# Gated attention of a two-layer decoder: scores inside blocks of 32 keys by small matmuls instead of 128-wide ones

## The chip, the cores and the metric

One core of a Trainium2 chip runs the whole forward pass of a two-layer decoder trunk for one sequence of 512 tokens (model width 1024). The metric is the device time of one execution in microseconds (us), given as the median of several runs. The trace that is read below is that of one profiled execution.

The engines are called by the names of the profile: PE is the matmul engine (PEld its loading of the stationary operand), DVE the vector engine, ACT the scalar engine, POOL a further vector engine that is almost unused here, and SP the queue that issues most DMAs. Each engine takes its instructions in order.

## The reference, cut to what matters

Layer 0 mixes tokens by gated linear attention with 4 heads, layer 1 by latent attention; each mixer is followed by a SwiGLU network, and every part is preceded by an RMS norm. What the change touches is the first mixer and the statistics of the norms:

```python
def gla_chunked(q, k, v, log_a):          # q, k, log_a (B,S,H,128), v (B,S,H,256)
    ...
    b = jnp.cumsum(gi, axis=-2)
    ...
    diff = b[:, :, :, None, :] - b[:, :, None, :, :]
    decay = jnp.exp(jnp.where(causal, diff, -jnp.inf))
    attn = jnp.einsum('bhik,bhjk,bhijk->bhij', qi, ki, decay)
    o_intra = jnp.einsum('bhij,bhjv->bhiv', attn, vi)

def rmsnorm(t, g):
    y = tf * lax.rsqrt(jnp.mean(tf * tf, axis=-1, keepdims=True) + EPS)
```

The score of a query i on a key j is a sum over 128 channels of q times k times a product of gates between j and i, one gate for each token and channel.

## The kernel before

All activations are kept transposed: channels on the 128 partitions, 512 tokens along the free dimension. Most matrix products are done in three matmuls on operands split into a high and a low part (`mm3`, L175 to L177), each 128 by 128 by 512. Weights arrive by SP in units of 128x1024 (`raw`), are rounded by ACT to `wh` (L161), and DVE subtracts to get `wl` (L169); three buffers of each rotate. In the first 265 us DVE also makes the modulation vectors of both layers from the weights `adaw` (L132): each is 512 KB, two buffers rotate, and DVE multiplies and sums one in L136 (`junk`).

**Scores of the gated attention.** For each head there is a tile `dg` of 128 keys by 4 times 128 queries: the diagonal blocks of the score matrix. It is filled in levels s = 1, 2, 4, ..., 64 (`LEVELS`). At level s, keys in an even group of s tokens meet queries in the odd group right after it, so that q and k, which `decay` (its two products are L580 and L581) multiplies by the gates of the groups after each level, carry the right product of gates. `head_setup` makes the diagonal itself: four matmuls of 128 keys by 128 queries, of which a product with the identity leaves the diagonal (L530). `level` (L548) does levels 1 to 16 with four matmuls a head, each of 128 keys by the 64 odd queries of a tile of 128 tokens (L556), and DVE copies the wanted entries through a mask `lm` (`copy_predicated`, L570). Levels 32 and 64 are done by `blocks` (L537): matmuls of only s keys by s queries (L542), whose output starts at partition b, and whose result DVE copies whole (L545). These operands are full fp32, and the trace has two records ("pieces" below) for each such matmul of the program.

**Order.** PE runs in an order that is written out by hand (`manual_schedule`). After the diagonals of heads 0 to 2 comes one unit of the v product, then the diagonal of head 3, then level 1 for the 4 heads, then a filler of 24 dense matmuls, level 2 for the 4 heads, a filler, and so on (`fill`). The fillers are units of the v product (`v_units`) and tiles of the gate (`r_tile`). DVE, ACT and SP are ordered by a scheduler from priorities and its own costs. ACT's order is by hand in the logs of the gates and in the first stretch of the program alone.

**Statistics of a norm.** `rstd_stats` (L216) sums squares over the channels: for each 128 tokens a matmul whose stationary operand is the tile `acc` of squares (128 tokens wide) and whose moving operand is one column of ones (L225); DVE then works out the inverse root on 128x4 numbers (L228, L203 to L212), and `rstd_spread` broadcasts it (L240). There are 15 such matmul groups: seven over all 512 tokens (first norm, four heads, `ckv`, `cq`), six over half the tokens, and two in the last norm over half the tokens with two operands each.

Of the kernel before, what the change touches and what calls it, by code (L numbers as in the profile page):

```python
# [18 lines left out]
P = 128  # L19
# [3 lines left out]
NT = S // P  # L23
# [17 lines left out]
FF_CHUNKS = ((0, 8), (8, 15), (15, 22))  # L41

LEVELS = (1, 2, 4, 8, 16, 32, 64)


C_ADAB = 0
# [10 lines left out]

K_ID = 0
K_CAUS = 128
NK_COL = 256  # L60

MAGIC = 12582912.0
TWO_PI = 6.283185307179586476925286766559
# [17 lines left out]
def trunk(ctx: ExitStack, tc: tile.TileContext, t: dict, out: bass.AP):  # L81
# [12 lines left out]
    def R(name, dt=F32, cols=S):  # L94
        return ring.tile([P, cols], dt, tag="ring", name=name, bufs=NRING)
# [7 lines left out]

    cols = cst.tile([P, NC_COL], F32, name="cols")
    kc = cst.tile([P, NK_COL], F32, name="kc")
    lm = cst.tile([P, 7 * 64], I32, name="lm")
    cact = cst.tile([P, D], F32, name="cact")
    x = [cst.tile([P, S], F32, name=f"x{k}") for k in range(KD)]
    ident = kc[:, K_ID:K_ID + P]
# [376 lines left out]
    def log_gates():  # L486
# [30 lines left out]
        for hd in range(H):  # L517
            et = R("et")
            nc.scalar.activation(out=et[:, :off], in_=tt[hd][:, :off], func=AF.Exp, scale=1.0 / TAU)
            heads[hd] = dict(e1=e1[hd], et=et, offs=offs)  # L520

    def head_setup(hd):
        d = heads[hd]
        qs, kr = qk[("q", hd)], qk[("k", hd)]
        dg = R("dg")
# [9 lines left out]
        d.update(kr=kr, qf=qf, dg=dg)  # L535

    def blocks(ps, kr, qf, dg, s):  # L537

        lo = range(0, P, 2 * s)
        for i in range(NT):  # L540
            for b in lo:
                nc.tensor.matmul(ps[b:b + s, i * s:(i + 1) * s], lhsT=kr[:, i * P + b:i * P + b + s],  # L542
                                 rhs=qf[:, i * P + b + s:i * P + b + 2 * s], start=i == 0, stop=i == NT - 1)
        for b in lo:
            nc.vector.tensor_copy(out=dg[b:b + s].rearrange("p (t a) -> p t a", t=NT)[:, :, b + s:b + 2 * s],  # L545
                                  in_=ps[b:b + s, :NT * s].rearrange("p (t a) -> p t a", t=NT))

    def level(hd, li, s):  # L548
        d = heads[hd]
        kr, qf, dg = d["kr"], d["qf"], d["dg"]  # L550
# [8 lines left out]
        na = 64 // s  # L559
        o = dg.rearrange("p (t a b s) -> p t a b s", t=NT, b=2, s=s)[:, :, :, 1, :]  # L560
        mk = lm[:, li * 64:(li + 1) * 64]
        dd = ps[:, :256]
        if 1 < s < 64:
            mk = mk.rearrange("p (a s) -> p a s", s=s)[:, None, :, :].to_broadcast([P, NT, na, s])
            dd = dd.rearrange("p (t a s) -> p t a s", t=NT, s=s)
        else:
            o = o.rearrange("p t a s -> p t (a s)")
            mk = mk[:, None, :].to_broadcast([P, NT, 64])
            dd = dd.rearrange("p (t a) -> p t a", t=NT)
        nc.vector.copy_predicated(out=o, mask=mk, data=dd)  # L570

    def decay(hd, s):
# [493 lines left out]
def _pack(inp):  # L1066
# [44 lines left out]
    kcv = np.zeros((P, NK_COL), np.float32)  # L1111
    kcv[:, K_ID:K_ID + P] = np.eye(P, dtype=np.float32)
    kcv[:, K_CAUS:K_CAUS + P] = np.where(np.arange(P)[None, :] > np.arange(P)[:, None], np.float32(-1e30), 0)
    d["kc"] = kcv
    j = np.arange(P)[:, None]
    lms = []
    for s in LEVELS:
        a = np.arange(64)[None, :] // s
        lms.append(((j // (2 * s) == a) & ((j // s) % 2 == 0)).astype(np.int32))
    d["lm"] = np.ascontiguousarray(np.concatenate(lms, axis=1))  # L1120

    gw = f("gla_w_in")[0]
# [62 lines left out]
```

## Time and profile before

| | us |
|---|---|
| median of 3 runs | 1202.94 (1202.93 to 1205.04) |
| the profiled execution, device time | 1200.87 |
| its span in the trace | 1199.1 |
| PE busy | 1168.8 (97% of the span) |
| DVE busy | 733.4 (61%) |
| ACT busy | 414.3 (35%) |
| POOL busy | 15.9 (1%) |

A matmul's end is modelled in the trace, so the pace of PE is read from the start of one row to the start of the next. A row with "x32" merges 32 neighbours of one line, and its length reaches to the modelled end of the last. The text in brackets at a row's end is the idle time of the engine before it and what ended it.

### The profile page before, as it was taken

To read this page: it belongs to the slowest core of one execution; us is meant where nothing else is said; L and a number is where in the kernel's file an instruction comes from. 1 tells how busy PE (TensorE), PEld (TensorE's weight loads), DVE (VectorE), ACT (ScalarE), POOL (GpSimd) and SP (SyncE) were. 2 spreads that over 40 slices of the span, in tenths; PEclk is the share of its full clock that TensorE was granted. 3 is DMA by queue.
4 is the path that set the end of the run, shared out by engine and by line. 5 is a ranking of instruction groups with operands and counts; after the bars stand their busy time and mean duration, and the time that the engine had idled before them with its cause. 6 is when DMAs were issued, how large, how long until landed. Compare 5 with 4: busy or idle time off the path is not lost.

```text
span 1199.1 us, 15412 instructions
## 1 busy us (share of the span) xinstructions
PE 1168.8 (97%) x6034; PEld 994.9 (83%) x6034; DVE 733.4 (61%) x1438; ACT 414.3 (35%) x652; POOL 15.9 (1%) x36
## 2 busy tenths in 40 slices
PE   6999999999999999999999999999999999999996
PEld 4778888899888888888899788989888888888886
DVE  7879888766664466756666778856433323333345
ACT  4272245343322232223344446634232123222231
POOL 0000000000000000000000022000000000000000
PEclk9999999999999999999999999999999999999998
DMA  8733454431674467447531133140323232233222
GB/s 295 269 102 106 146 193 143 144 135 56 220 239 152 136 232 235 161 151 251 184 99 45 57 82 91 36 151 8 106 88 106 88 105 84 92 106 105 84 75 71
DMA packets 47370, 156.82 MB, mean 131 GB/s; under 512 B 5601, under 2 KB 8033, under 8 KB 47298
## 3 DMA queue, kind: packets, MB, share of 16 engines
q1 hardware_dynamic: 45474, 153.54, 38.7%
q0 software_dynamic: 1536, 2.10, 0.8%
q8 instruction: 47, 0.77, 0.3%
q10 hardware_dynamic: 288, 0.21, 0.1%
q14 instruction: 25, 0.20, 0.1%
HBM read 151.63 MB, written 2.10 MB: 128 GB/s over the span
## 4 chain that ended last, share of the span: by engine, by line
PE 87%; DVE 6%; DMA 4%; ACT 1%; issue 1%; ACTq 0%; DVEq 0%
PE f L177 12%; PE f L176 12%; PE f L175 12%; PE op L175 8%; PE op L177 8%; PE op L176 8%; DMA adaw<-in_ada 2%; PE fg L176 2%; PE fg L177 2%; PE fg L175 2%; PE lv L556 1%; DVE junk L136 1%; DVE wl L169 1%; PE v L175 1%; DMA raw<-in_gla_wo 1%; PE v L177 1%
## 5 line engine op out<-in xcount | busy, mean ns | idle before, releaser
L161 ACT CAST wh<-raw 128x1024 fp32r<-128x1024 f32 (+2 forms) x181 | 185.7, 1027 | 581.3 <-PE f L176 180.1
L169 DVE TENSOR_TENSOR wl<-raw,wh 128x1024 fp32r<-128x1024 f32 (+2 forms) x181 | 215.1, 1190 | 113.2 <-ACT wh L161 106.9
L176 PE MATMUL f<-hl,wh 128*128 128x512 f32 x640 | 249.2, 389 | 0.0
L175 PE MATMUL f<-hh,wh 128*128 128x512 f32 x640 | 249.2, 389 | 0.0
L177 PE MATMUL f<-hh,wl 128*128 128x512 f32 x640 | 249.1, 389 | 0.0
L175 PE MATMUL op<-acth,wh 128*128 128x512 f32 (+1 forms) x394 | 144.8, 367 | 0.0
L176 PE MATMUL op<-actl,wh 128*128 128x512 f32 (+1 forms) x394 | 144.5, 367 | 0.0
L177 PE MATMUL op<-acth,wl 128*128 128x512 f32 (+1 forms) x394 | 144.5, 367 | 0.0
L176 PEld LDWEIGHTS f<-hl,wh 128*128 128x128 f32 x640 | 120.2, 188 | 25.0
L175 PEld LDWEIGHTS f<-hh,wh 128*128 128x128 f32 x640 | 120.2, 188 | 24.9
L177 PEld LDWEIGHTS f<-hh,wl 128*128 128x128 f32 x640 | 120.2, 188 | 24.7
L284 DVE SCALAR_TENSOR_TENSOR x<-op,mod,x 128x512 f32<-128x512 f32 (+1 forms) x76 | 50.5, 665 | 123.4 <-PE op L177 123.0
L136 DVE SCALAR_TENSOR_TENSOR junk<-adaw,cact 128x1024 bf16<-128x1024 f32 x96 | 117.1, 1219 | 12.4 <-DMA adaw<-in_ada 12.0
L797 DVE TENSOR_TENSOR sg<-sg,f 128x512 f32<-128x512 f32 x40 | 27.5, 687 | 126.7 <-PE f L177 126.7
L176 PEld LDWEIGHTS op<-actl,wh 128*128 128x128 f32 x394 | 74.3, 189 | 12.2
L175 PEld LDWEIGHTS op<-acth,wh 128*128 128x128 f32 x394 | 74.3, 189 | 12.2
L177 PEld LDWEIGHTS op<-acth,wl 128*128 128x128 f32 x394 | 74.3, 189 | 12.0
L274 ACT ACTIVATE hh<-u,mod 128x256 fp32r<-128x256 f32 (+1 forms) x56 | 28.6, 536 | 54.9 <-DVE u L271 38.8
L262 DVE TENSOR_TENSOR acc<-acc,sq 128x512 f32<-128x512 f32 (+1 forms) x52 | 29.9, 576 | 17.0 <-ACT sq L261 16.5
L261 ACT ACTIVATE sq<-x 128x512 f32<-128x512 f32 (+1 forms) x45 | 23.6, 525 | 39.8 <-DVE x L284 37.7
L275 DVE SCALAR_TENSOR_TENSOR hl<-u,mod,hh 128x256 fp32r<-128x256 f32 (+1 forms) x56 | 27.8, 519 | 12.1 <-ACT hh L274 12.1
L799 DVE TENSOR_TENSOR actl<-sg,acth 128x512 fp32r<-128x512 f32 (+1 forms) x48 | 30.7, 640 | 0.8 <-ACT acth L798 0.5
(307 smaller groups left out, 1907.0 us busy)
## 6 DMA issues: line engine op xcount, KB each, us to landing
adaw<-in_ada SPq DMA_DIRECT2D x96, 512.0 KB, 4.2
raw<-in_ffn_in SPq DMA_DIRECT2D x80, 512.0 KB, 3.5
raw<-in_ffn_o SPq DMA_DIRECT2D x32, 448.0 KB, 3.3
raw<-in_ffn_o SPq DMA_DIRECT2D x16, 512.0 KB, 3.6
raw<-in_gla_ko SPq DMA_DIRECT2D x8, 512.0 KB, 4.6
raw<-in_gla_v SPq DMA_DIRECT2D x8, 512.0 KB, 3.5
raw<-in_gla_r SPq DMA_DIRECT2D x8, 512.0 KB, 3.6
raw<-in_gla_wo SPq DMA_DIRECT2D x8, 512.0 KB, 4.9
```

The lines of the kernel that those rows point to most:

```text
L136: nc.vector.scalar_tensor_tensor(out=junk, in0=w, scalar=1.0, in1=cact, op0=ALU.mult, op1=ALU.mult, accum_out=acc)
L161: nc.scalar.copy(out=wh[:, :n], in_=raw[:, :n])
L169: ins = nc.vector.tensor_tensor(out=wl[:, :n], in0=raw[:, :n], in1=wh[:, :n].bitcast(F32), op=ALU.subtract)
L175: nc.tensor.matmul(ps, lhsT=ah, rhs=bh, start=start, stop=False)
L176: nc.tensor.matmul(ps, lhsT=ah, rhs=bl, start=False, stop=False)
L177: nc.tensor.matmul(ps, lhsT=al, rhs=bh, start=False, stop=stop)
L262: nc.vector.tensor_tensor(out=self.acc[:, c], in0=self.acc[:, c], in1=sq[:, c], op=ALU.add)
L274: nc.scalar.activation(out=hi[:, c], in_=u[:, c], func=AF.Identity, bias=sh)
L275: ins = nc.vector.scalar_tensor_tensor(out=lo[:, c], in0=u[:, c], scalar=sh, in1=hi[:, c].bitcast(F32), op0=ALU.add, op1=ALU.subtract)
L284: ins = nc.vector.scalar_tensor_tensor(out=x[k][:, c], in0=ps[:, c], scalar=mod[l][2 + 3 * j][:, k:k + 1], in1=x[k][:, c], op0=ALU.mult, o ...
L797: ins = nc.vector.tensor_tensor(out=sg[:, c], in0=sg[:, c], in1=pu[:, c], op=ALU.mult)
L799: nc.vector.tensor_tensor(out=lo[:, c], in0=sg[:, c], in1=hi[:, c].bitcast(F32), op=ALU.subtract)
```

## The change

The diagonal and the levels 1 to 16 stay inside blocks of 32 tokens. The change computes only these: for each 32 keys one matmul of 32 keys by the 32 queries (diagonal) or by the 16 odd queries (levels) of their own block, with the output at partitions b = 0, 32, 64, 96 and the matching `tile_position`. The results lie densely in a tile `dq`, 128 partitions by 128 numbers a head, which all four heads share. Masks and masked copies shrink to 128x64. At level 32 the tile `dg` is allocated, cleared by POOL, and ACT copies the four blocks of `dq` into it; levels 32 and 64 go on as before. The statistics of all norms do 32 tokens a matmul in place of 128.

```diff
+QB = 32
...
-    lm = cst.tile([P, 7 * 64], I32, name="lm")
+    lm = cst.tile([P, 5 * 64], I32, name="lm")
...
-                    nc.tensor.matmul(st[:, i:i + 1], lhsT=acc[:, c.start + i * P:c.start + (i + 1) * P], rhs=ones,
-                                     start=m == 0 and i == 0, stop=m == len(accs) - 1 and i == n - 1)
+                    for b in range(0, P, QB):
+                        o = c.start + i * P + b
+                        nc.tensor.matmul(st[b:b + QB, i:i + 1], lhsT=acc[:, o:o + QB], rhs=ones,
+                                         start=m == 0 and i == 0, stop=m == len(accs) - 1 and i == n - 1,
+                                         tile_position=(0, b))
...
         for i in range(NT):
-            c = slice(i * P, (i + 1) * P)
-            nc.tensor.matmul(ps[:, c], lhsT=kr[:, c], rhs=qs[:, c], start=(i == 0), stop=(i == NT - 1))
-        nc.vector.tensor_tensor(out=dg.rearrange("p (a b) -> p a b", b=P),
-                                in0=ps.rearrange("p (a b) -> p a b", b=P),
-                                in1=ident[:, None, :].to_broadcast([P, NT, P]), op=ALU.mult)
+            for b in range(0, P, QB):
+                c = slice(i * P + b, i * P + b + QB)
+                nc.tensor.matmul(ps[b:b + QB, i * QB:(i + 1) * QB], lhsT=kr[:, c], rhs=qs[:, c],
+                                 start=i == 0, stop=i == NT - 1, tile_position=(0, b))
+        nc.vector.tensor_tensor(out=dq.rearrange("p (a b) -> p a b", b=QB),
+                                in0=ps[:, :NT * QB].rearrange("p (a b) -> p a b", b=QB),
+                                in1=kc[:, None, K_IDQ:K_IDQ + QB].to_broadcast([P, NT, QB]), op=ALU.mult)
...
-        if s >= 32:
-            return blocks(ps, kr, qf, dg, s)
+        if s >= QB:
+            if s == QB:
+                d["dg"] = R("dg")
+                nc.gpsimd.memset(d["dg"], 0.0)
+                for b in range(0, P, QB):
+                    nc.scalar.copy(out=d["dg"][b:b + QB].rearrange("p (t a) -> p t a", t=NT)[:, :, b:b + QB],
+                                   in_=dq[b:b + QB].rearrange("p (t a) -> p t a", t=NT))
+            return blocks(ps, kr, qf, d["dg"], s)
+        nq = QB // 2
         for i in range(NT):
-            c = slice(i * P, (i + 1) * P)
-            nc.tensor.matmul(ps[:, i * 64:(i + 1) * 64], lhsT=kr[:, c],
-                             rhs=qf[:, c].rearrange("p (a b s) -> p a b s", b=2, s=s)[:, :, 1, :],
-                             start=(i == 0), stop=(i == NT - 1))
...
+            for b in range(0, P, QB):
+                c = slice(i * P + b, i * P + b + QB)
+                nc.tensor.matmul(ps[b:b + QB, i * nq:(i + 1) * nq], lhsT=kr[:, c],
+                                 rhs=qf[:, c].rearrange("p (a b s) -> p a b s", b=2, s=s)[:, :, 1, :],
+                                 start=i == 0, stop=i == NT - 1, tile_position=(0, b))
```

On PE, at level 4 (between a unit of the v product and a tile `r` of the gate), this stood:

```order
L176 MATMUL v_719<-wl,hh 128x512
L177 MATMUL v_719<-wh,hl 128x512
L556 MATMUL lv<-qf,k 128x64 x16
L175 MATMUL r<-hh,wh 128x512
L176 MATMUL r<-hl,wh 128x512
L177 MATMUL r<-hh,wl 128x512
```

and with the change this:

```order
L178 MATMUL v_731<-wl,hh 128x512
L179 MATMUL v_731<-wh,hl 128x512
L577 MATMUL lv<-qf,k 32x16 x64
L177 MATMUL r<-hh,wh 128x512
L178 MATMUL r<-hl,wh 128x512
L179 MATMUL r<-hh,wl 128x512
```

Nothing moved on PE: 64 matmuls with an output of 32x16 take the place of 16 with one of 128x64, four heads together.

On ACT, between the activation of the second gate tile (`sr`) and the first split of the scores (`ah`), this stood:

```order
L161 CAST wh<-raw 128x1024
L673 ACTIVATE sr<-r 128x512
L161 CAST wh<-raw 128x1024 x2
L296 CAST ah<-dg 128x4x128 x2
L161 CAST wh<-raw 128x1024
```

and with the change this:

```order
L163 CAST wh<-raw 128x1024
L686 ACTIVATE sr<-r 128x512
L570 COPY dg<-dq 32x4x32 x16
L163 CAST wh<-raw 128x1024 x2
L301 CAST ah<-dg 128x4x128 x2
L163 CAST wh<-raw 128x1024
```

The sixteen copies stand ahead of two roundings of weights.

On DVE the scheduler also gives another order in the stretch of the first product (20 to 65 us), where the modulation of x by `gs`, `u`, `hl` alternates with the work on `adaw` (`junk`) and `wl`. For channel tiles 2 and 3 (x_85 and x_86) this stood:

```order
L136 SCALAR_TENSOR_TENSOR junk,adac<-adaw,cact 128x1024
L146 SCALAR_TENSOR_TENSOR gs_0_121<-mod_1_110,cols 128x1
L138 TENSOR_TENSOR mod_0_109<-adac,cols 128x1
L271 SCALAR_TENSOR_TENSOR u<-x_86,gs_0_121,rstd 128x512
L136 SCALAR_TENSOR_TENSOR junk,adac<-adaw,cact 128x1024
L275 SCALAR_TENSOR_TENSOR hl<-u,mod_0_109,hh 128x512
L138 TENSOR_TENSOR mod_1_110<-adac,cols 128x1
L169 TENSOR_TENSOR wl<-raw,wh 128x1024
```

and with the change this:

```order
L276 SCALAR_TENSOR_TENSOR u<-x_86,gs_0_121,rstd 128x512
L171 TENSOR_TENSOR wl<-raw,wh 128x1024
L138 SCALAR_TENSOR_TENSOR junk,adac<-adaw,cact 128x1024
L140 TENSOR_TENSOR mod_0_109<-adac,cols 128x1
L280 SCALAR_TENSOR_TENSOR hl<-u,mod_0_109,hh 128x512
L138 SCALAR_TENSOR_TENSOR junk,adac<-adaw,cact 128x1024
L171 TENSOR_TENSOR wl<-raw,wh 128x1024
```

`hl` of channel tile 3 now stands ahead of the following `junk`, where it stood behind it, and one `wl` stands ahead of that pair.

## Rows read from the trace of the kernel before

**Rows 1.** Busy time, share of the span and instructions of each engine (page).

```profile
PE 1168.8 (97%) x6034; PEld 994.9 (83%) x6034; DVE 733.4 (61%) x1438; ACT 414.3 (35%) x652; POOL 15.9 (1%) x36
```

**Rows 2.** Chain that ended last, shares by engine (page).

```profile
PE 87%; DVE 6%; DMA 4%; ACT 1%; issue 1%; ACTq 0%; DVEq 0%
```

**Rows 3.** Windows between levels: length, then busy us of PE, PEld, DVE, ACT, POOL.

```profile
95.01:104.06 9.05, 9.05 (x58) 8.07 (x58) 9.05 (x20) 1.05 (x1) 0.00 (x0) 1.00 0.34 103
113.12:122.15 9.03, 9.03 (x58) 8.09 (x58) 7.70 (x21) 2.93 (x3) 0.00 (x0) 1.00 0.37 114
```

**Rows 4.** Timeline of PE, 82 to 146 us: start, length, engine, line, operation.

```profile
82.26 2.84 PE L529 MATMUL lv<-q,k 128*128 128x128 f32 x24
84.85 0.48 PE L175 MATMUL v<-wh,hh 128*128 128x512 f32 x1
...
90.39 1.05 PE L529 MATMUL lv<-q,k 128*128 128x128 f32 x8
...
95.01 0.48 PE L175 MATMUL v<-wh,hh 128*128 128x512 f32 x1
...
109.64 3.68 PE L556 MATMUL lv<-qf,k 128*128 128x64 f32 x32
113.12 0.48 PE L175 MATMUL r<-hh,wh 128*128 128x512 f32 x1
...
136.52 0.39 PE L177 MATMUL v<-wh,hl 128*128 128x512 f32 x1
136.84 1.21 PE L542 MATMUL lv<-qf,k 128*32 128x32 f32 x64
137.97 0.50 PE L175 MATMUL v<-wh,hh 128*128 128x512 f32 x1
...
143.64 2.08 PE L542 MATMUL lv<-qf,k 128*64 128x64 f32 x32
145.65 0.50 PE L175 MATMUL v<-wh,hh 128*128 128x512 f32 x1
```

**Rows 5.** Timeline of DVE, 88 to 130 us.

```profile
88.51 0.67 DVE L481 COPY k<-qk 128x512 f32<-128x512 f32 x1
89.11 0.67 DVE L530 TENSOR_TENSOR dg<-lv,kc 128x512 f32<-128x512 f32 x1
...
128.76 0.43 DVE L570 COPY_PREDICATED dg<-lm,lv 128x256 f32<-128x256 int32 x1 [2.62 <-PE lv L556]
129.10 0.42 DVE L580 TENSOR_TENSOR qf<-qf,et 128x256 f32<-128x256 f32 x1
```

**Rows 6.** Timeline of ACT, 136 to 171 us.

```profile
136.99 1.05 ACT L161 CAST wh<-raw 128x1024 fp32r<-128x1024 f32 x1 [7.71 <-issue]
...
170.26 0.36 ACT L296 CAST ah<-od_a 128x256 fp32r<-128x256 f32 x1
```

**Rows 7.** Timeline of PE at three statistics.

```profile
172.99 1.02 PE L225 MATMUL no_st<-ones,acc 128*128 128x1 f32 x8 [1.06 <-DVE acc L262]
173.88 0.48 PE L175 MATMUL r<-hh,wh 128*128 128x512 f32 x1
...
258.98 0.50 PE L225 MATMUL nm_st<-ones,acc 128*128 128x1 f32 x4
259.35 0.36 PE L175 MATMUL op<-ohh,wh 128*128 128x256 f32 x1
...
1178.99 0.51 PE L225 MATMUL nf_st<-ones,acc 128*128 128x1 f32 x4
1179.81 0.36 PE L175 MATMUL op<-acth,wh 128*128 128x256 f32 x1
```

**Rows 8.** Timeline of DVE, then of PE, 11 to 42 us.

```profile
13.74 0.16 DVE L228 TENSOR_SCALAR rs_v<-n_st 128x4 f32<-128x4 f32 x1
...
39.30 1.23 DVE L136 SCALAR_TENSOR_TENSOR junk<-adaw,cact 128x1024 bf16<-128x1024 f32 x1 [1.11 <-DMA adaw<-in_ada]
...
41.25 0.50 PE L176 MATMUL ko<-hl,wh 128*128 128x512 f32 x1 [0.58 <-DVE hl L275]
```

More of the change, by code (lines that the diff above doesn't have):

```diff
@@ L59 @@
 K_CAUS = 128
-NK_COL = 256
+K_IDQ = 256
+NK_COL = 288
 MAGIC = 12582912.0
@@ L520, in log_gates @@
             heads[hd] = dict(e1=e1[hd], et=et, offs=offs)
+    dqs = []
     def head_setup(hd):
@@ L524, in head_setup @@
         qs, kr = qk[("q", hd)], qk[("k", hd)]
-        dg = R("dg")
+        if not dqs:
+            dqs.append(R("dq"))
+        dq = dqs[0][:, hd * NT * QB:(hd + 1) * NT * QB]
         ps = abank("lv0")
         for i in range(NT):
-            c = slice(i * P, (i + 1) * P)
-            nc.tensor.matmul(ps[:, c], lhsT=kr[:, c], rhs=qs[:, c], start=(i == 0), stop=(i == NT - 1))
-        nc.vector.tensor_tensor(out=dg.rearrange("p (a b) -> p a b", b=P),
-                                in0=ps.rearrange("p (a b) -> p a b", b=P),
-                                in1=ident[:, None, :].to_broadcast([P, NT, P]), op=ALU.mult)
+            for b in range(0, P, QB):
[5 more added lines that the diff above has]
+                                in1=kc[:, None, K_IDQ:K_IDQ + QB].to_broadcast([P, NT, QB]), op=ALU.mult)
         qf = R("qf")
         nc.vector.tensor_tensor(out=qf, in0=qs, in1=d["e1"], op=ALU.mult)
-        d.update(kr=kr, qf=qf, dg=dg)
+        d.update(kr=kr, qf=qf, dq=dq)
     def blocks(ps, kr, qf, dg, s):
@@ L542, in blocks @@
                 nc.tensor.matmul(ps[b:b + s, i * s:(i + 1) * s], lhsT=kr[:, i * P + b:i * P + b + s],
-                                 rhs=qf[:, i * P + b + s:i * P + b + 2 * s], start=i == 0, stop=i == NT - 1)
+                                 rhs=qf[:, i * P + b + s:i * P + b + 2 * s], start=i == 0, stop=i == NT - 1,
+                                 tile_position=(0, b))
         for b in lo:
@@ L549, in level @@
         d = heads[hd]
-        kr, qf, dg = d["kr"], d["qf"], d["dg"]
+        kr, qf, dq = d["kr"], d["qf"], d["dq"]
         ps = abank("lv")
-        if s >= 32:
-            return blocks(ps, kr, qf, dg, s)
-        for i in range(NT):
-            c = slice(i * P, (i + 1) * P)
-            nc.tensor.matmul(ps[:, i * 64:(i + 1) * 64], lhsT=kr[:, c],
-                             rhs=qf[:, c].rearrange("p (a b s) -> p a b s", b=2, s=s)[:, :, 1, :],
-                             start=(i == 0), stop=(i == NT - 1))
[L559 to L569, printed above, removed]
+        if s >= QB:
[7 more added lines that the diff above has]
+        nq = QB // 2
+        for i in range(NT):
+            for b in range(0, P, QB):
[3 more added lines that the diff above has]
+                                 start=i == 0, stop=i == NT - 1, tile_position=(0, b))
+        o = dq.rearrange("p (a b s) -> p a b s", b=2, s=s)[:, :, 1, :]
+        mk = lm[:, li * 64:(li + 1) * 64].rearrange("p (a s) -> p a s", s=s)
+        dd = ps[:, :NT * nq].rearrange("p (a s) -> p a s", s=s)
         nc.vector.copy_predicated(out=o, mask=mk, data=dd)
@@ L1113, in _pack @@
     kcv[:, K_CAUS:K_CAUS + P] = np.where(np.arange(P)[None, :] > np.arange(P)[:, None], np.float32(-1e30), 0)
+    kcv[:, K_IDQ:K_IDQ + QB] = np.arange(P)[:, None] % QB == np.arange(QB)[None, :]
     d["kc"] = kcv
@@ L1116, in _pack @@
     lms = []
-    for s in LEVELS:
-        a = np.arange(64)[None, :] // s
-        lms.append(((j // (2 * s) == a) & ((j // s) % 2 == 0)).astype(np.int32))
+    for s in LEVELS[:5]:
+        a = np.arange(QB // 2)[None, :] // s
+        lms.append(np.tile((j % QB // (2 * s) == a) & ((j // s) % 2 == 0), (1, NT)).astype(np.int32))
     d["lm"] = np.ascontiguousarray(np.concatenate(lms, axis=1))
```

## The prediction

> **What bounds the kernel now.** I read the page first. PE is busy for 97% of the span [rows 1], and the chain of waits followed back from the end lies on PE for 87% [rows 2]. So what counts is PE's time in the stretches that the change touches, as long as the engines that feed it keep up there. Next come the windows between levels: in the period of level 2 PE is busy for all 9.05 us, and so is DVE; two periods later DVE is busy for 7.70 of 9.03 us [rows 3]. PE is the bound, but at the first levels DVE has nothing to spare. Then the timeline of PE gives the price of each kind of matmul, and that of DVE shows whom it waits for: at level 16 it sat idle for 2.62 us until PE delivered [rows 5], so DVE follows PE there.
>
> **The price of a piece.** The same kernel already has matmuls of the new kind. Level 32 (32 keys by 32 queries, partitions 0 and 64 in turn) runs 64 pieces from 136.84 to 137.97, which is 17.7 ns a piece. Level 64 (64 by 64, always at partition 0) runs 32 pieces from 143.64 to 145.65, or 62.8 ns [rows 4]. Half of that, 31.4 ns, is what a piece of 32 columns would cost if neighbours did not overlap. The new matmuls have the width of level 32 and also change their place at every step (0, 32, 64, 96), so I take 17.7 ns; 31.4 ns is the upper bound. The lower bound is half of 17.7, if four places overlap twice as well as two do.
>
> Entering such a group costs a little: a dense filler has 24 matmuls between 84.85 and 90.39, so 0.23 us each, but the last one before level 32 starts 0.32 us ahead of it (136.52 to 136.84) [rows 4]. I charge 0.09 us a group.
>
> The Trainium skill, TensorE: Matmul & The Clock Gate, section on the 56 ns gap, says that starts never come closer than about 25 ns however small the moving operand is. Here the trace disagrees: level 32 shows 17.7 ns. By that rule the whole sum below would be 0.5 us; it is a rival below.
>
> **The levels.** One level for four heads takes 3.48 us now (109.64 to 113.12, 32 pieces) [rows 4]. After the change it has 64 matmuls, so 128 pieces: 128 x 17.7 ns + 0.09 = 2.36 us. That saves 1.12 us, and 4.5 us over levels 2, 4, 8 and 16.
>
> The diagonal and level 1 lie in two stretches. Heads 0 to 2 of the diagonal take 2.59 us (82.26 to 84.85) and would take 96 x 17.7 ns + 0.09 = 1.79. Head 3 and level 1 take 4.62 us (90.39 to 95.01) and would take 160 x 17.7 ns + 0.09 = 2.92 [rows 4]. PE alone would save 2.5 us. But level 1 needs `qf`, and DVE comes to that work only after its copy of k, at 89.11. There it alternates `dg` and `qf`, 0.60 us each (the step from 88.51 to 89.11 is that of 512 numbers a partition; 256 numbers take 0.34, from 128.76 to 129.10) [rows 5]. A straight line through the two gives 0.21 us for the 128 numbers of `dq`, so the last `qf` is done at 89.11 + 4 x 0.81 = 92.35. PE then has the last head of level 1 to do, 0.57 us, and is through at about 93.0 instead of 95.01. I take 2.0 us of the 2.5. If DVE's small operations did not shrink at all, it would be 93.9 and 0.5 us.
>
> After that DVE keeps up. Masked copies shrink from 256 to 64 numbers, by the same line from 0.34 to 0.15 us. Level 1's twelve operations then take 4 x (0.15 + 0.34 + 0.34) = 3.3 us and end at 95.7, while PE comes to level 2 at 93.0 + 5.5 = 98.5. Later a period of PE lasts 5.5 + 2.36 = 7.9 us, and DVE needs 7.70 - 4 x 0.19 = 6.9. So the levels give 6.5 us.
>
> **What the copies add.** Sixteen copies on ACT at level 32: a cast of 256 numbers a partition took 0.36 us [rows 6], so 128 numbers cost at most that; nothing is the lower bound; with 0.25 us they take 4 us. They can begin with level 16's masked copies. ACT had been idle for 7.71 us before the rounding of weights at 136.99 [rows 6], which covers even 16 x 0.36 = 5.8 us. If that cover were gone, the two roundings that stand behind them would be late, but with three buffers they serve fillers two periods on. So I cost them at nothing. POOL's four clearings have no row of their size; DVE's 0.67 us for 512 numbers [rows 5] as the price makes 2.7 us. POOL has no other work in this stretch, and the places it clears become free when the gates' exponentials are done, ahead of level 1, which leaves five periods. Nothing again; without that cover DVE's copies of level 32 would wait for them.
>
> **The statistics.** Over all tokens a group takes 0.89 us (172.99 to 173.88) and would take 32 x 17.7 ns + 0.09 = 0.66. Over half the tokens it takes 0.37 (258.98 to 259.35) and would take 0.37. In the last norm it is 0.82 (1178.99 to 1179.81) against 0.66 [rows 7]. Six full groups save 1.4 us, the six halves nothing, the two last ones 0.3. The first norm's group I count at nothing: DVE took up its result at 13.74 with no idle time before [rows 8], straight from other work, so an earlier result waits. Together 1.7 us.
>
> **The new order in the first product.** Before, DVE waited 1.11 us for a load of `adaw` at 39.30, with `hl` of channel tile 3 queued behind it, and PE waited for that `hl` until 41.25 [rows 8]. Now `hl` and a `wl` go ahead of that `junk`, and PE can start up to 1.8 us earlier. But the `hl` of each later tile still stands behind a `junk` whose load is asked for only when an earlier `junk` frees one of two buffers, and those now start no sooner: what PE gains at tile 3 it waits for at tile 4. I take nothing, with bounds of 1.8 us gained and 1.2 us (one `junk` more in the way) lost. The smaller `lm` and larger `kc` are one DMA each and count as nothing.
>
> **Sum.** 4.5 + 2.0 + 1.7 = 8.2 us. The profiled execution took 1200.87 us and should become 1192.7. It was 2.07 us below the median of the runs shown; on the median 1202.94 the forecast is 1194.7 us.
>
> **Rivals.** All of them can be read from one line: with p ns a piece, levels, diagonal and statistics together save 28.5 - 1.12 p us (the 512 + 256 + 352 new pieces, against what those stretches take now less the entries), of which DVE withholds 0.5 at 17.7. The sum is zero at 25.5 ns.
> - *The groups of 32 do not overlap, and the kernel gets slower.* At 31.4 ns a piece, a level takes 4.1 us instead of 3.48, and all together loses 6.5 us: 1209.4. For it: level 64, whose matmuls stay in one place, pays by columns. Against it: level 32 does overlap, and the new order never stays in one place for two matmuls. It decides from 25.5 ns on.
> - *The change doesn't do what it says.* A floor for a piece, which level 32 passed only over its short stretch of 1.13 us, cancels it: halfway between the two paces (24.6 ns) 0.9 us are left, so 1202.0. The skill's 25 ns is this case. Against it: 64 pieces in a row kept the pace.
> - *The gain is taken back later.* At 172.99 PE waits 1.06 us for DVE's `acc` [rows 7]. If DVE's work ahead of that is paced by loads of `adaw` and not by PE, PE only arrives earlier at the same wait: the 6.5 us of the levels are gone, 1201.2. For it: such waits exist [rows 8]. Against it: DVE idled for PE at level 16 [rows 5], so it was ahead, and it has less to do now.
> - *Four places overlap better than two.* At 8.9 ns the line gives 18.6 us; DVE holds level 1 back to 92.35 + 0.28 and so withholds 2.4: 1186.7.
>
> **How the numbers follow.** The forecast's own case has 0.72; with a pace between 15 and 21 ns (3.6 us either way) and the first product's bounds it spans about 1190 to 1199. No overlap has 0.07, the floor 0.08, the gain taken back 0.06, four places better 0.07. A measurement of this kernel can tell about 0.2%, or 2.4 us, from no change: faster holds the first and the last, 0.79; same the floor and the late wait, 0.14; slower 0.07. From 1189 to 1201 lie the forecast's case and part of its neighbours, 8 in 10.
>
> **What would show it.** In the profile after: each of levels 2 to 16 near 2.36 us from its first piece to the next filler, and a period near 7.9 us; the last `qf` ahead of level 1 ends its wait on PE; the sixteen copies on ACT end before level 32 begins; full statistics near 0.66 us. The prediction is wrong if the pace of 128x16 pieces is not that of level 32, if PE waits for DVE between levels or longer than 1.06 us at the first head's statistics, or if the first product ends by more than 2 us elsewhere than it did.

## The result, and the profile after

The changed kernel takes 1185.22 us (median of 4 runs, 1184.10 to 1187.90) against 1203.42 us for the kernel before (4 runs, 1202.93 to 1205.04). The ratio is 0.987, with a 95% interval of 0.9853 to 0.9886: 13.7 to 17.7 us faster. The forecast was 1194.7, 8.2 us faster. The profiled execution took 1184.1 us, its span 1182.3.

The page of the changed kernel: busy time, then the shares of the chain of waits. Beside [rows 1, 2], PE is busy for 20 us less, with 864 more records (432 more matmuls of two pieces each), and it still holds most of the chain; DVE's share of it has grown from 6% to 8%.

```profile
PE 1148.6 (97%) x6898; PEld 971.8 (82%) x6898; DVE 725.9 (61%) x1438; ACT 419.0 (35%) x668; POOL 18.0 (2%) x40
...
PE 85%; DVE 8%; DMA 3%; ACT 2%; issue 1%; ACTq 0%; DVEq 0%
```

The windows of the same two periods as in [rows 3] (length, then busy time of PE, PEld, DVE, ACT, POOL, then granted clock, DMA share and GB/s):

```profile
93.26:100.19 6.93, 6.93 (x161) 5.67 (x152) 6.92 (x18) 1.05 (x1) 0.00 (x0) 1.00 0.29 83
107.13:114.13 7.00, 7.00 (x160) 5.72 (x153) 6.74 (x19) 2.29 (x4) 0.00 (x0) 1.00 0.25 92
```

A period has shrunk by 2.1 and 2.0 us, nearly twice what was forecast (9.05 to 7.9). DVE is busy for nearly all of both; in the second it was busy for 7.70 of 9.03 us before.

The timeline of PE, the counterpart of [rows 4]:

```profile
82.81 1.05 PE L539 MATMUL lv<-q,k 128*32 128x32 f32 x96
83.79 0.50 PE L177 MATMUL v<-wh,hh 128*128 128x512 f32 x1
...
90.49 0.45 PE L577 MATMUL lv<-qf,k 128*32 128x16 f32 x32 [0.43 <-DVE qf L545]
...
92.89 0.45 PE L577 MATMUL lv<-qf,k 128*32 128x16 f32 x32 [0.35 <-DVE qf L545]
93.26 0.50 PE L177 MATMUL v<-wh,hh 128*128 128x512 f32 x1
...
98.61 0.39 PE L179 MATMUL v<-wh,hl 128*128 128x512 f32 x1
98.93 1.34 PE L577 MATMUL lv<-qf,k 128*32 128x16 f32 x128
100.19 0.50 PE L177 MATMUL v<-wh,hh 128*128 128x512 f32 x1
...
126.74 1.23 PE L553 MATMUL lv<-qf,k 128*32 128x32 f32 x64
127.90 0.50 PE L177 MATMUL v<-wh,hh 128*128 128x512 f32 x1
...
133.57 2.08 PE L553 MATMUL lv<-qf,k 128*64 128x64 f32 x32
135.58 0.50 PE L177 MATMUL v<-wh,hh 128*128 128x512 f32 x1
```

From its first piece to the next dense matmul level 2 takes 1.26 us (98.93 to 100.19) where 2.27 was forecast, which is 9.8 ns for each of 128 pieces. Levels 32 and 64, which the change leaves alone, cost what they did. Level 32 starts at 126.74 instead of 136.84. At level 1 all four heads wait for DVE's `qf` (0.43 us and three times 0.35), as forecast.

The statistics, the counterpart of [rows 7]:

```profile
162.69 0.43 PE L229 MATMUL no_st<-ones,acc 128*32 128x1 f32 x32 [0.83 <-DVE acc L267]
163.05 0.50 PE L177 MATMUL r<-hh,wh 128*128 128x512 f32 x1
...
246.02 0.31 PE L229 MATMUL nm_st<-ones,acc 128*32 128x1 f32 x16
246.25 0.38 PE L177 MATMUL op<-ohh,wh 128*128 128x256 f32 x1
...
1162.88 0.31 PE L229 MATMUL nf_st<-ones,acc 128*32 128x1 f32 x16
1163.24 0.38 PE L177 MATMUL op<-acth,wh 128*128 128x256 f32 x1
```

They take 0.36, 0.23 and 0.36 us, where 0.89, 0.37 and 0.82 stood, and about 0.09 us more to enter each.

One part of the difference between the two profiled executions is probably not the change's. At the query product of layer 1, behind waits of 1.43 and 0.83 us of PE, the granted clock fell in the execution of before, from 2.4 GHz to a mixture with 1.2. In the changed kernel PE waits there too (1.42 and 0.85 us), and the clock stayed. The windows of PE there, of before and then of the changed kernel (length, busy time, granted clock, DMA share, GB/s):

```profile
684.00:690.00 6.00, 5.71 (x18) 0.72 0.21 66
```

```profile
670.00:676.00 6.00, 5.84 (x26) 1.00 0.22 68
```

The query product itself takes 6.91 us before (682.95 to 689.86) and 5.33 in the changed kernel (668.82 to 674.15): 1.6 us for the clock. From the query statistics (670.79 and 657.05) to the first scores of layer 1 that need `qst` (700.84 and 684.76) the changed kernel takes 27.7 us instead of 30.05, 1.9 us more than its statistics save; the rest of that is a wait for the DMA of `qst`, 0.37 us instead of 0.74.

The fall came in 7 of the 16 profiles of this study: in all three that have the 128-wide levels (before twice, and with the new statistics alone) and in four of the other thirteen. The few profiles don't exclude that the kernel has a part in it. Over all executions on record, though, the mean granted clock is 0.995 for both kernels (26 of before, 8 of the changed one, from 0.993 to 0.997), so the medians owe the clock little, wherever it falls.

### The profile page after: what moved, and what is told of

It reads as the page before. It is cut to its first block, busy times and chain, and to the rows that moved or that the text cites. A ratio compares the mean times of both kernels' runs of the same rounds, so it can differ in the third digit from the quotient of the medians.

```text
span 1182.3 us, 17166 instructions
## 1 busy us (share of the span) xinstructions
PE 1148.6 (97%) x6898; PEld 971.8 (82%) x6898; DVE 725.9 (61%) x1438; ACT 419.0 (35%) x668; POOL 18.0 (2%) x40
## 4 chain that ended last, share of the span: by engine, by line
PE 85%; DVE 8%; DMA 3%; ACT 2%; issue 1%; ACTq 0%; DVEq 0%
PE f L179 12%; PE f L178 12%; PE f L177 12%; PE op L177 9%; PE op L178 9%; PE op L179 9%; DMA adaw<-in_ada 2%; PE fg L178 2%; PE fg L177 2%; PE fg L179 2%; DVE junk L138 2%; DVE wl L171 1%; PE r L177 1%; PE r L178 1%; PE r L179 1%
## 5 line engine op out<-in xcount | busy, mean ns | idle before, releaser
L138 DVE SCALAR_TENSOR_TENSOR junk<-adaw,cact 128x1024 bf16<-128x1024 f32 x96 | 117.2, 1221 | 13.7 <-DMA adaw<-in_ada 13.4
L178 PEld LDWEIGHTS op<-actl,wh 128*128 128x128 f32 x394 | 74.3, 189 | 12.2
L177 PEld LDWEIGHTS op<-acth,wh 128*128 128x128 f32 x394 | 74.3, 188 | 12.2
L279 ACT ACTIVATE hh<-u,mod 128x256 fp32r<-128x256 f32 (+1 forms) x56 | 28.6, 537 | 54.8 <-DVE u L276 31.4
```

The lines of the kernel that those rows point to most:

```text
L138: nc.vector.scalar_tensor_tensor(out=junk, in0=w, scalar=1.0, in1=cact, op0=ALU.mult, op1=ALU.mult, accum_out=acc)
L177: nc.tensor.matmul(ps, lhsT=ah, rhs=bh, start=start, stop=False)
L178: nc.tensor.matmul(ps, lhsT=ah, rhs=bl, start=False, stop=False)
L279: nc.scalar.activation(out=hi[:, c], in_=u[:, c], func=AF.Identity, bias=sh)
```

## The experiments

The theory (a place is the 32 output partitions, 0, 32, 64 or 96, that a matmul writes): pieces at different places run side by side, and the price of a piece falls with the number of other places that are visited before its own comes again; four places in turn are therefore cheaper than level 32's two. The first rival: the new pieces are cheap because they are small (16 queries instead of 32). The second: part of the gain lies elsewhere (statistics, waits, clock).

### Statistics of 128 tokens

```diff
-                    for b in range(0, P, QB):
-                        o = c.start + i * P + b
-                        nc.tensor.matmul(st[b:b + QB, i:i + 1], lhsT=acc[:, o:o + QB], rhs=ones,
+                    nc.tensor.matmul(st[:, i:i + 1], lhsT=acc[:, c.start + i * P:c.start + (i + 1) * P], rhs=ones,
```

> Levels and diagonal in blocks of 32, statistics of the norms in groups of 128 tokens as before the change. In the changed kernel a full group of statistics takes 0.36 us to the next matmul (162.69 to 163.05), a half 0.23 (246.02 to 246.25) and the last norm's pair 0.36; before it was 0.89, 0.37 and 0.82. If the four places are what made the statistics cheap, this kernel gets those times of before again and loses 6 x 0.53 + 6 x 0.14 + 0.46 = 4.5 us: about 1189.7. If the statistics are worth only what the prediction gave them (1.7 us), it takes about 1186.9. A further 1.8 us hangs on the granted clock at the query product of layer 1, which fell to half in the profiled run of the kernel before and stayed full in that of the changed one: if the statistics of 128 tokens had anything to do with that, the clock falls here as well.

Measured: 1190.08 us (4 runs), ratio to before 0.9913 (0.9898 to 0.9928). That is 4.9 us above the changed kernel. The rows of the statistics give 4.5, or 3.3 with the 0.09 us more that each group takes to enter; this run and the one with the new statistics alone (4.0, below) can't tell these apart, but 1.7 is too little. In this profile the clock at the query product stayed full, so the old statistics did not make it fall.

### Two places, one place, wider pieces

The order of the pieces in the diagonal and levels 1 to 16, two places at a time, and one at a time:

```diff
-        for i in range(NT):
-            for b in range(0, P, QB):
+        for b, i in ((b + o, i) for b in (0, 2 * QB) for i in range(NT) for o in (0, QB)):
```

```diff
-        for i in range(NT):
-            for b in range(0, P, QB):
+        for b in range(0, P, QB):
+            for i in range(NT):
```

> Diagonal and levels 1 to 16 with the same 32-key pieces, but in an order that alternates between two places only (0, 32, 0, 32, ... for the four tiles, then 64, 96, 64, 96, ...). Theory of the places: each place takes about 35 ns a piece and places work side by side, so two of them give level 32's pace of 17.7 ns and a level of four heads takes 128 x 17.7 ns + 0.09 = 2.36 us instead of 1.37; levels 2 to 16 lose 4.0 us, the first three diagonals 0.7, and level 1 nothing, since DVE paces it: about 1190. Rival: pieces are cheap because they are small (32 keys by 16 queries), wherever they lie: a level stays at 1.37 us and the time at 1185.

> Diagonal and levels 1 to 16 with the same pieces, all four tiles of one place in a row, then the next place. Theory of the places: neighbours do not overlap but at three changes of place in 16 pieces, so a piece costs 31 to 35 ns (half of level 64's 62.8, or twice level 32's 17.7), less a fifth for the changes of place: a level of four heads takes 3.3 to 4.4 us, about what the 128-wide matmuls took (3.48). The levels 2 to 16 then lose 8 to 12 us, the diagonal 2, and level 1 about 0.5: near 1198, with 1195 to 1201 as the range. Rival of the small pieces: 1.37 us a level and 1185.

And all 32 queries of a block as the moving operand:

```diff
-                nc.tensor.matmul(ps[b:b + QB, i * nq:(i + 1) * nq], lhsT=kr[:, c],
-                                 rhs=qf[:, c].rearrange("p (a b s) -> p a b s", b=2, s=s)[:, :, 1, :],
+                nc.tensor.matmul(ps[b:b + QB, i * QB:(i + 1) * QB], lhsT=kr[:, c], rhs=qf[:, c],
```

> Levels 1 to 16 with all 32 queries of a block as the moving operand instead of the 16 odd ones, at four places as in the changed kernel; the even queries' scores are computed too and not used. If a piece's price at a place is the same for 16 and 32 columns (level 32, two places, 32 columns: 17.7 x 2 = 35 ns; levels, four places, 16 columns: 9.9 x 4 = 40 ns), a level stays at 1.3 to 1.4 us and the time at 1185. If the price goes by columns, which would mean that the narrower pieces and not the four places made the gain, a level takes up to 2.6 us and the time is up to 5 us longer: 1190.

Measured: 1186.62 us with two places, 1189.26 with one, 1185.73 with wider pieces (4 runs each; before on that chip 1200.69). PE's timeline, first of two places (the first three diagonals, then level 2), then level 2 with one place and with wider pieces:

```profile
82.08 1.29 PE L538 MATMUL lv<-q,k 128*32 128x32 f32 x96
83.30 0.50 PE L177 MATMUL v<-wh,hh 128*128 128x512 f32 x1
...
98.91 1.63 PE L575 MATMUL lv<-qf,k 128*32 128x16 f32 x128
100.47 0.50 PE L177 MATMUL v<-wh,hh 128*128 128x512 f32 x1
```

```profile
98.19 2.73 PE L577 MATMUL lv<-qf,k 128*32 128x16 f32 x128
100.85 0.50 PE L177 MATMUL v<-wh,hh 128*128 128x512 f32 x1
```

```profile
99.89 1.37 PE L577 MATMUL lv<-qf,k 128*32 128x32 f32 x128
101.18 0.50 PE L177 MATMUL v<-wh,hh 128*128 128x512 f32 x1
```

A level takes 1.56, 2.66 and 1.29 us, against 1.26: 12.2, 20.8 and 10.1 ns a piece. Twice the columns cost 3%, so the small pieces are not the reason. The order alone moves the price by a factor of two, so the places are. Both sizes that I had expected were too high, though: two places cost 12.2 and not level 32's 17.7, and one place 20.8 and not 31 to 35. The columns don't explain the first miss: the diagonal has level 32's 32 columns and costs 12.7 ns at two places (82.08 to 83.30). With one place, level 1 ended half a us later, as expected: 4.95 us after DVE began the copy of `k` (87.58 to 92.53) instead of 4.42 (88.84 to 93.26), and PE did not wait for `qf`.

### Which two places, and how often the pair changes

In these orders "four" and "eight" count matmuls, each of two pieces. First the pair 0 and 64, then 32 and 96, with level 32 itself doing its four tiles at place 0 and then four at 64; then the pairs 0 and 32, then 64 and 96, changing after four matmuls instead of eight:

```diff
+        for b, i in ((b + o, i) for b in (0, QB) for i in range(NT) for o in (0, 2 * QB)):
...
-        for i in range(NT):
-            for b in lo:
+        for b in lo:
+            for i in range(NT):
```

```diff
+        for b, i in ((b + o, j + i) for j in (0, 2) for b in (0, 2 * QB) for i in range(2) for o in (0, QB)):
```

> Two places at a time as in the run with two places, but the pair 0 and 64 (then 32 and 96), which is the pair that level 32 uses; and level 32 itself in the slow order (its four tiles at place 0, then those at 64). If the distance of the two places is why level 32 pays 17.8 ns a piece and the two-place levels only 12.2, a level now takes 128 x 17.8 ns = 2.28 us. If it is the change of pair after every eight pieces (pieces of the next pair start while those of the last are still running), a level stays at 1.56 us. Level 32 in the slow order should go from 1.16 to 1.3 to 1.4 us by the one-place price of 20.8 ns.

> Two places at a time (0 and 32, then 64 and 96), but the pair changes after every four pieces instead of eight. If pieces overlap whenever a neighbour lies at another place, and a change of pair gives such a neighbour, the level comes closer to the 1.26 us of four places: 1.35 to 1.45 us against 1.56. If only the number of places in turn counts, it stays at 1.56.

Measured: 1189.30 and 1185.68 us (one run each). PE's timeline, of the first run (level 2, then level 32):

```profile
100.95 1.63 PE L575 MATMUL lv<-qf,k 128*32 128x16 f32 x128
102.50 0.50 PE L177 MATMUL v<-wh,hh 128*128 128x512 f32 x1
...
129.83 1.51 PE L552 MATMUL lv<-qf,k 128*32 128x32 f32 x64
131.28 0.50 PE L177 MATMUL v<-wh,hh 128*128 128x512 f32 x1
```

and of the second (level 4):

```profile
105.64 1.42 PE L575 MATMUL lv<-qf,k 128*32 128x16 f32 x128
106.99 0.50 PE L177 MATMUL r<-hh,wh 128*128 128x512 f32 x1
```

The distance of the two places does not matter: 1.55 us. The change of pair does: 1.35 us (10.5 ns; 1.34 to 1.40 over the four levels) when it comes twice as often. Level 32 at one place takes 1.45 us (22.7 ns) instead of 1.16 (18.1). So all prices fall in one row, by how often the next piece finds its place free: 9.8 ns with four places in turn, 10.5 and 12.2 with pairs that change after four and eight matmuls, 18 with one pair for good, 21 to 23 with four matmuls in a row at one place.

The start times of the single pieces in the traces show it directly. In the changed kernel's level 32 (one pair) they follow each other by 7 and 25 ns in turn, so two pieces in 32 ns. In the first head of its level 2 (four places) they follow by 7, 7, 6 and 12 ns, so four pieces in 32 ns. In the order with one place they lie 31 or 32 ns apart, or go 5 and 27 in turn, I infer around a change of place (the trace does not name a piece's place). So in each order a place takes a piece about every 32 ns. Behind the first head of the four-place level gaps of 29 to 45 ns come in (8.6 ns a piece in that head, 10.1 and 9.1 in the next two); why was not tried.

### Every level twice

```diff
-        for i in range(NT):
+        for i in (*range(NT), *range(NT)):
```

> Every level's matmuls are issued twice (the second pass overwrites the scores with the same numbers), and so are those of the statistics with a single sum; the sums of these statistics come out twice as large where the second pass adds up. What a level gains in length, divided by its number of pieces, is the price of a piece without what it costs to enter and leave the group. Theory of the places: the four-place price is half of the two-place price of level 32. With the changed kernel's 1.26 us a level for 128 pieces and 1.16 us for the 64 pieces of level 32, and a cost of entering and leaving of 0.1 to 0.25 us in both, the added time is 1.0 to 1.15 us a level (8 to 9 ns a piece) and 0.9 to 1.05 us at level 32 (14 to 16.5 ns). Rival: there is no such fixed cost and four places give 9.8 against 18.1 ns. If the stretch in which level 32 kept its pace had been too short for a slower steady pace to show (the floor of the prediction, 25 ns), the added pass would take 3.2 us a level and 1.6 us at level 32.

Measured: 1209.19 us (one run). Level 32 takes 2.15 us (146.88 to 149.03) instead of 1.16, so 15.5 ns a piece that is added; the 25 ns floor is out. The four-place price could not be had this way, because PE stopped once in each doubled level from 1 to 16, for 1.9 to 2.7 us, for nothing that the profile shows. The timeline and the waits of PE:

```profile
104.79 2.43 PE L577 MATMUL lv<-qf,k 128*32 128x16 f32 x234
109.29 0.38 PE L577 MATMUL lv<-qf,k 128*32 128x16 f32 x22 [2.07 <-issue]
...
146.88 2.22 PE L553 MATMUL lv<-qf,k 128*32 128x32 f32 x128
149.03 0.50 PE L177 MATMUL v<-wh,hh 128*128 128x512 f32 x1
```

```profile
PE lv L577 <- issue: 10.6, 5, 2.7
```

In level 2, 234 pieces take 2.43 us up to the stop against 128 in 1.34, so the 106 further ones cost 10.3 ns each by these rows (9.4 to 11.3 by those of the later levels): not clearly less than 9.8. That four places halve level 32's price exactly is thereby not confirmed.

The stops do not go by the length of a level: they come after 132, 234, 208, 182 and 156 of its pieces. Counted from one stop to the next, the trace has 769, 512, 511 and 512 instructions of PE and PEld, dense matmuls included. So the stops go by the number of instructions (the kernels without doubled levels have none); what brings the next ones was not tried.

### Level 64 at two places

```diff
+                for o in range(b, b + s, QB):
+                    nc.tensor.matmul(ps[o:o + QB, i * s:(i + 1) * s], lhsT=kr[:, i * P + o:i * P + o + QB],
```

> Level 64 of the changed kernel is one matmul of 64 keys by 64 queries a tile, always at place 0: 32 of them take 2.00 us. Here each is two of 32 keys by 64 queries, at places 0 and 32 in turn. Theory of the places, with a price at a place that does not go by columns (16 and 32 columns cost the same in the run with wider pieces): 64 pieces at 12 to 18 ns, so 0.8 to 1.2 us, and about 1184.2 in all. If 64 columns cost twice what 32 do, two places only win back the doubled number of pieces: about 2.0 us, and no change.

Measured: 1184.49 us (4 runs; before on that chip 1201.53), within the scatter of the changed kernel. In PE's timeline level 64 goes from 2.01 to 1.91 us:

```profile
134.34 1.98 PE L554 MATMUL lv<-qf,k 128*32 128x64 f32 x64
136.25 0.50 PE L177 MATMUL v<-wh,hh 128*128 128x512 f32 x1
```

Here columns do count: 29.8 ns a piece with 64 of them, against 18 with 32 (level 32), which is also at one pair of places.

### Four products on POOL

```diff
-        nc.vector.tensor_tensor(out=qf, in0=qs, in1=d["e1"], op=ALU.mult)
+        nc.gpsimd.tensor_tensor(out=qf, in0=qs, in1=d["e1"], op=ALU.mult)
```

> The four products qf, which at level 1 of the changed kernel end PE's waits (0.43 and three times 0.35 us), are done by POOL instead of DVE. If DVE's row of dq and qf is what holds PE at level 1, PE is through with it at about 91.6 instead of 93.26 and the kernel gains up to 1.6 us (1183.6), provided POOL is done with the last qf by 90.5; its inputs are there from 84.8 on, so it may take 1.4 us for each. POOL's clearing of as many numbers takes 0.53 us. Rival: POOL takes 2 us or more for each, or the two engines slow each other down; then PE waits for POOL until 93 or later and nothing is gained.

Measured: 1189.13 us (4 runs; before on that chip 1201.53), 3.9 us slower than the changed kernel. The timelines of POOL, DVE and PE in this run, and of DVE in the changed kernel:

```profile
82.79 6.96 POOL L545 TENSOR_TENSOR qf<-q,e 128x512 f32<-128x512 f32 x4 [82.35 <-ACT e L510]
...
82.99 7.68 DVE L518 TENSOR_TENSOR tt<-tt 128x128 f32<-128x128 f32 x28
...
93.61 0.66 PE L539 MATMUL lv<-q,k 128*32 128x32 f32 x32 [4.66 <-DVE k L486]
```

```profile
83.58 3.09 DVE L518 TENSOR_TENSOR tt<-tt 128x128 f32<-128x128 f32 x28
```

POOL was done with the last `qf` at 89.75, in time. But DVE's 28 sums beside it took 7.68 us instead of 3.09, so its copy of `k` came late and PE waited 4.66 us for that. Only four of the 28 were longer, those of 128x16: 1.30 to 1.33 us each instead of 0.18. They and POOL's products took turns: the sums start at 84.76, 85.99, 87.24 and 88.49 and last until POOL's next product or its first clearing has begun (86.01, 87.25, 88.50 and 89.71). POOL's first product, beside the wider sums, lasted 3.24 us, the other three 1.26 to 1.28. The Trainium skill, GPSIMD Engine Reference, section Specifications, says that the two engines share their interface to SBUF, with contention for DVE's instructions with two SBUF inputs; these sums have two, and the trace agrees.

### Level 1 without waits

Half of level 1's filler ahead of level 1 (first), and level 1 and head 3's diagonal in the slow order (second; the cut shows level 1), beside the changed kernel run again (third):

```diff
+                if g == 0 and u == 2 and kk == 0:
+                    yield
...
         head_setup(H - 1)
+        next(v0)
```

```diff
+        for i, b in (((i, b) for b in range(0, P, QB) for i in range(NT)) if s == 1 else
+                     ((i, b) for i in range(NT) for b in range(0, P, QB))):
```

> The changed kernel with one half of level 1's filler (12 of 24 dense matmuls) moved ahead of level 1. In the changed kernel PE waits 0.43 and three times 0.35 us for DVE's qf at level 1, and in the profiles of three of its variants (128-token statistics, wider pieces, level 64 split) the granted clock fell to about half of full right behind level 1, which made the filler after it 6.9 to 7.2 us long instead of 5.67; in the changed kernel's own profile and in the two whose level 1 was slower it did not. If those waits are the cause of both, PE now comes to level 1 about 2.8 us later, when DVE has the qf ready: no waits, level 1 in 1.3 us, the clock full behind it, and 1.4 us gained against an execution without the dip, 2.7 against one with it: about 1183.5. Rival: DVE is the bound from there to level 32 (busy 96% of it), so what PE gains at level 1 it waits for at level 2 or 4: 1185.

> The changed kernel, but the diagonal of head 3 and level 1 in the slow order (the four tiles of one place in a row); levels 2 to 16 stay at four places. The pieces of level 1 then take 0.65 us a head, close to DVE's step of 0.80, and PE is busy there instead of waiting. If DVE sets the end of level 1, the slower order costs nothing there, and if PE's idle time is what lets the clock fall behind it, the clock stays at 1.00: 1184 to 1185, no slower than the changed kernel. Rival: the price of pieces counts at level 1 too: 4 x 0.34 us more, so 1186.5.

> The changed kernel once more beside these three, for a comparison on one chip and a second profile: 1184 to 1187, a level again 1.26 us from its first piece to the filler; the clock behind level 1 and at the query product of layer 1 is full or falls to half by chance.

Measured: 1186.06 (1183.10 to 1188.00), 1184.20 (1183.37 to 1185.96) and 1184.89 us (1183.55 to 1187.95), 4 runs each, with 1200.91 for before on that chip: the three cannot be told apart, and the 1183.5 expected of the half filler was not reached. The windows of PE at and behind level 1 show what moved, of the half filler, the slow order and the changed kernel again:

```profile
93.00:95.00 2.00, 2.00 (x132) 1.00 0.20 18
```

```profile
93.00:95.00 2.00, 2.00 (x10) 1.00 0.00 0
```

```profile
91.00:93.00 2.00, 1.54 (x66) 0.82 0.20 74
93.00:95.00 2.00, 2.00 (x6) 0.50 0.00 0
```

In the changed kernel's second profile the clock stood at 1.2 GHz (0.50) behind level 1, and the way from there to level 2 took 7.23 us (92.29 to 99.52) instead of 5.67. Eight profiles have a level 1 that waits for `qf` (those of the doubled levels and of the products on POOL are left out); in five of them the clock fell there. In none of the six with a busy level 1 did it fall there. That points to the waits, but the half filler and the slow order have one profile each, and in two further runs of the half filler the mean granted clock was 0.993 and 0.994, lower than in the changed kernel's four on that chip (0.995 and 0.996); where it fell in them no trace shows. From the diagonal's start to level 32 the half filler needs 42.5 us, the slow order 44.7, and the changed kernel 43.9 and 45.5 in its two profiles. The time of the whole does not show this above its scatter; whether the half filler is the better kernel stays open.

### The parts by themselves

The kernel before with the new statistics alone, and the kernel before once more:

> The kernel before with the statistics of all norms in blocks of 32 and nothing else of the change. By the groups' times in the two profiles (0.89 to 0.36 six times, 0.37 to 0.23 six times, 0.82 to 0.36 once) this gains 4.5 us against the kernel before; by the prediction's 17.7 ns a piece it gains 1.7.

> The kernel before once more, for a second profile. In its first profile the granted clock fell to 0.73 in a stretch of 5 us at the query product of layer 1 (685 to 690); in the changed kernel's it stayed at 1.00 there, which makes some 1.8 us of the 16.8 us between these two executions. The same dip came back in the run with two places (0.66) and stayed away in the three others, so I take it for a chance of the single execution: here it comes or stays away, and the levels take 3.48 us each as before.

Measured: the kernel with the new statistics alone takes 1196.89 us (6 runs) against 1200.91 of before on that chip, ratio 0.9961 (0.9945 to 0.9978), 4.0 us. The second execution of before took 1202.96 us; its levels cost what they did (3.49 us from 100.99 to 104.48), and the clock fell at the query product again (0.66 over 686 to 691).

## Why the prediction was wrong

**The failed step is the price of a piece.** I wrote that the new matmuls "have the width of level 32 and also change their place at every step (0, 32, 64, 96), so I take 17.7 ns". The runs showed 9.8 ns in its place, and 1185.22 us lies below the range of 1189 to 1201. The mechanism was right (places overlap) and so, within about a microsecond, was the line that I read the rivals from; the price put into it was off. With 9.8 ns it gives 28.5 - 1.12 x 9.8 = 17.5 us, less the 2.4 that DVE withholds, so 15.1 us, inside the measured 13.7 to 17.7; its three terms measured 14.0 in the table below. The case "four places overlap better than two", to which I gave 0.07, is what happened. I treated level 32's price as that of any change of place, where it is that of going back and forth between two. Width, the other half of the argument, counted for nothing up to 32 columns; nor was it the same, as the levels' new matmuls have 16 moving columns and level 32's have 32.

**Term by term**, between the two profiled executions:

| term | forecast | measured |
|---|---|---|
| levels 2 to 16 | 4.5 | 4 x (3.48 - 1.28 - 0.09) = 8.4 |
| diagonal and level 1 | 2.0 | 12.75 - 10.45 = 2.3 |
| statistics, entries included | 1.7 | 6 x 0.44 + 6 x 0.05 + 0.37 = 3.3 |
| first product | 0 | 82.26 to 82.81: -0.5 |
| granted clock at the query product | 0 | 1.6, probably not the change's |

(1.28 is the mean of the four levels; 12.75 and 10.45 run from the first piece of the diagonal to level 1's filler.) That makes 15.1 of 16.8 us; 0.4 more is the shorter wait for `qst`, and where the other 1.3 us lie was not traced. The first product ends within 0.5 us of where it ended (81.84 in the changed kernel's second profile): PE no longer waits at 41 us, but 0.57 us at 47.22 for the next `hl`, as forecast. The halves of the statistics, at nothing in the forecast, gain by the lower price too: 16 pieces in 0.23 us instead of the 0.28 that 17.7 ns make. Of the last norm's two groups, which the forecast both counted, only the first saves: at the second PE waits for ACT's `sq` either way (0.68 us before, 0.79 now).

**DVE at level 1** was right in kind and nearly in size. The timeline of DVE:

```profile
89.45 0.30 DVE L541 TENSOR_TENSOR dq<-lv,kc 128x128 f32<-128x128 f32 x1
89.64 0.70 DVE L545 TENSOR_TENSOR qf<-q,e 128x512 f32<-128x512 f32 x1
...
92.05 0.70 DVE L545 TENSOR_TENSOR qf<-q,e 128x512 f32<-128x512 f32 x1
92.64 0.31 DVE L583 COPY_PREDICATED dq<-lm,lv 128x64 f32<-128x64 int32 x1
92.78 0.44 DVE L593 TENSOR_TENSOR qf<-qf,e 128x256 f32<-128x256 f32 x1
...
127.30 0.58 DVE L557 COPY dg<-lv 32x128 f32<-32x128 f32 x2 [1.14 <-PE lv L553]
```

`dq` steps 0.20 us (forecast 0.21), the masked copy 0.14 (0.15), the last `qf` ends at 92.64 (92.35), and PE is through at 93.26 (93.0). That DVE keeps up afterwards holds too: at 127.30 it idles for PE. At level 2 it is busy for 6.92 of 6.93 us, but it was busy for all 9.05 before as well [rows 3] and PE lost nothing to it, so whether a further saving on PE there would meet DVE is not shown.

**The copies on ACT and the clearings on POOL** were hidden. POOL is done with its four by 87.86, long before level 32 (126.74). The sixteen copies take 0.31 us each and end 0.7 us before level 32 begins:

```profile
121.12 4.93 ACT L570 COPY dg<-dq 32x128 f32<-32x128 f32 x16
```

**The other rivals.** *No overlap* falls twice: the order with the least overlap still costs 20.8 ns, below the break-even of 25.5, and the kernel with it is at 1189.26, faster than before. The upper bound of 31.4 ns, half of level 64's price, is close to what single pieces at one place show (starts 31 or 32 ns apart); but no order of 32-key pieces here stays at one place for more than four matmuls, and each change of place wins some of it back. *The floor* falls by the 9.8 ns and by the doubled level 32 (15.5 ns). The Trainium skill, TensorE: Matmul & The Clock Gate, section on the 56 ns gap, has starts no closer than about 25 ns; these runs measured 9.8 on average, and 31 or 32 only between pieces at one place. The Trainium skill, TensorE: Matmul & The Clock Gate, Part 3 on packing small matmuls, has three column places finish 2.38 times as fast as without packing; here four places gained 20.8 / 9.8 = 2.1 over the order that stays for four matmuls. That part speaks for the case that came true, and I had not weighed it. *The gain taken back later* did not come: PE waits 0.83 us at 162.69, less than the 1.06 of [rows 7].

## What to carry to other kernels

Before pricing a small matmul by one that is already in the kernel, ask what its neighbours are: the same piece cost 9.8 or 20.8 ns by nothing but the order of its loop. Small matmuls that write different places belong in an order that visits as many places as possible before coming back. And where another engine paces PE, speed gained there is lost; in five of eight profiles with such waits the granted clock fell right behind them, which cost more, though the time of the whole did not show it.

## What the runs showed of the hardware that was not expected

- Pieces of 16 and of 32 columns cost nearly the same at four places (9.8 and 10.1 ns); with 64 columns a piece cost 29.8 ns at two places, against 18 with 32.
- One place took a piece of 16 or 32 columns about every 32 ns, and another place its own 5 to 7 ns later.
- Waits of 0.18 to 0.43 us between the heads of level 1 were followed by 1.2 GHz in five of eight profiles, at a price of 1.6 us in the one shown above.
- With every level doubled, PE stopped for 1.9 to 2.7 us each time 511 or 512 more instructions (matmuls and loads) had gone by, the first time 769; the profile names only "issue", and what was late was not tried. None of the other fifteen profiles has such a stop.
- Four products on POOL and the sums on DVE beside them took turns: four sums of 128x16 took 1.3 us instead of 0.18.
